# VectorE computes 1024 rank-one updates of the MLP's second product, and GpSimd makes the low parts of the MLP's weights

## The chip, the cores and the metric

The kernel runs on one core of one Trainium2 chip. The metric is the device time of one execution in microseconds (us), as the median of several runs. The engines are TensorE (PE, with its weight loads shown as PEld), VectorE (DVE), ScalarE (ACT), GpSimd (POOL) and SyncE (SP), whose queue issues nearly all of this kernel's DMAs.

## The reference

One decoder layer is applied to 256 prompt positions and 8 x 4 sampled positions, 288 tokens in all, with 2048 channels and float32 data:

```
h = rmsnorm(x)
proj = h @ w_in + b_in                    # 2048 -> 3072
mix = concat(conv group, pooling group)   # 1024 + 1024
x = x + mix @ w_out                       # 2048 -> 2048
h2 = rmsnorm(x)
f = square(relu(h2 @ w_ff1))              # 2048 -> 8192
x = x + f @ w_ff2                         # 8192 -> 2048
y = rmsnorm(x)
```

New convolution and pooling states are outputs too. The change touches the last two products, the MLP.

## The kernel before

Channels lie on the 128 partitions and the 288 tokens (`T`) along the free dimension. `xT` holds the residual x as 16 blocks of 128 x 288.

A float32 product is made of three TensorE products of rounded parts. Each operand is split into a high part and a low part (the remainder), and `product` (L279 to L284) adds high x high, high x low and low x high into one PSUM bank. The weights are split while they stream in. `split` (L270 to L277) takes a raw tile of 128 x 1024 numbers (four weight blocks for each of two output blocks), lets ScalarE copy it to the high part `whi` (L275), and lets an engine that the caller names subtract to get the low part `wlo` (L276). `weight_groups` (L308) names that engine. In the first stages, the input projection, the pooling product and the first half of the output product, it is GpSimd (`G`). In the second half of the output product and in the whole MLP it is VectorE (`V`, L327 and L329).

A `gemm` (L286) makes two output blocks of 128 channels from 16 blocks of input channels: 16 x 2 products of three matmuls, 96 matmuls of 128 x 288, and four weight tiles. The pool of raw tiles holds six, the pools of `whi` and `wlo` four each, so the split of a tile for the next gemm waits until PE has read the tile that lay in its place. PSUM gives the gemms four banks, two for each, so a gemm can start once the bank pair of the gemm before the last has been read.

The MLP (L565) has four chunks of 2048 hidden channels. A chunk is eight gemms of the first product (FF1) and eight of the second (FF2). After an FF1 gemm, VectorE makes `t` from the bank (L574), ScalarE squares it into `f` (L576) and copies the high part `fh`, and VectorE makes `fl` (L579). After an FF2 gemm, VectorE adds the two banks to their blocks of `xT` (L589, the function `evict`). Between the output product and the MLP, GpSimd splits a row of sums (`parts`, L232 and L233, into `th` and `tl`) for the second norm.

The order of instructions on each engine is set by a scheduler when the program is built. It simulates the engines and takes, of what is ready, what has the lowest priority number. Code inside `with later():` gets a number a million higher, so it is placed where its engine would otherwise have nothing to do. All DMAs of weights are issued from the one queue of SP, in order, and each waits there until its raw tile is free.

Of the kernel before, what the change touches and what calls it, by code (L numbers as in the profile page):

```python
# [9 lines left out]
F32 = mybir.dt.float32  # L10
F32R = mybir.dt.float32r
AF = mybir.ActivationFunctionType
ALU = mybir.AluOpType
# [3 lines left out]
P = 128  # L17
# [3 lines left out]
T = SEQ + NB * NS  # L21
# [8 lines left out]
N8 = DC // P  # L30
WINDOWS = (2, 4, 8, 16)
FCH = 2048
US = CH + NS
UO = CH + SEQ
UL = UO + NB * US
ZS = PH + NS
# [5 lines left out]

GROUPS = (3, 2, 1, 0)
SEQUENCE = [("conv", i) for i in range(2, 7)] + [("pool", 3), ("pool", 2), ("pool", 1), ("mix", 3), ("pool", 0), ("mix", 2), ("conv", 7)]


def weight_blocks():

    def w_in(*cols):
        return [("w_in", r, cols) for r in range(0, D, 1024)]  # L50

    a, b = [w_in(i * P, DC + i * P) for i in range(2)]
    yield from (a[0], b[0], a[1], b[1])
    for kind, i in SEQUENCE:
        if kind == "mix":
            if i == 3:
                yield "pool_w", 0, (0, P)
            continue
        yield from w_in(i * P, DC + i * P) if kind == "conv" else w_in(2 * DC + 2 * i * P, 2 * DC + (2 * i + 1) * P)
    for r in (DC, 0):  # L60
        for c in range(0, D, 256):
            yield "w_out", r, (c, c + P)
    for ch in range(0, DFF, FCH):
        for c in range(ch, ch + FCH, 256):
            for r in range(0, D, 1024):
                yield "w_ff1", r, (c, c + P)
        for c in range(0, D, 256):
            for r in range(ch, ch + FCH, 1024):
                yield "w_ff2", r, (c, c + P)
# [12 lines left out]
def trunk_kernel(ctx: ExitStack, tc: tile.TileContext, io):  # L82
    nc = tc.nc
# [5 lines left out]
    actp = ctx.enter_context(tc.tile_pool(name="actp", bufs=40))  # L89
    tmpp = ctx.enter_context(tc.tile_pool(name="tmpp", bufs=6))  # L90
    prdp = ctx.enter_context(tc.tile_pool(name="prdp", bufs=1))
    acc = ctx.enter_context(tc.tile_pool(name="acc", bufs=4, space=PSUM))
    cvp = ctx.enter_context(tc.tile_pool(name="cvp", bufs=2, space=PSUM))
    msp = ctx.enter_context(tc.tile_pool(name="msp", bufs=2, space=PSUM))
# [7 lines left out]
    @contextmanager  # L102
    def later(by=LATER):

        tc.cur_priority += by
        yield
        tc.cur_priority -= by

    def row(name):
        return rowp.tile([P, T], F32, name=nm(name), tag="row")  # L110
# [4 lines left out]
    def act(name, **kw):  # L115
        return slot(name, F32R, **(kw or {"tag": "act"}))
# [4 lines left out]
    def ms(name, n=512):  # L121
        return msp.tile([P, n], F32, name=nm(name), tag="ms", padded_shape=[P, 512])
# [17 lines left out]
    xT = const.tile([P, KT, T], F32, name="xT")  # L140
    uz = const.tile([P, N8 * (UL + ZL)], F32, name="uz")
# [12 lines left out]
    def load():  # L154

        src = io["w"][next(next_block)]
        raws = []
        for h in range(2):
            raw = raw_tile()
            nc.sync.dma_start(raw, src[:, 4 * h : 4 * h + 4, :])  # L160
            raws.append(raw)
        return raws
# [107 lines left out]
    def split(raw, eng, cuts=((0, 4),)):  # L270

        hi = wspl.tile([P, 4, 256], F32R, name=nm("whi"), tag="whi")
        lo = wspl.tile([P, 4, 256], F32R, name=nm("wlo"), tag="wlo")
        for a, b in cuts:
            nc.scalar.copy(hi[:, a:b, :], raw[:, a:b, :])  # L275
            eng.tensor_tensor(lo[:, a:b, :], raw[:, a:b, :], hi[:, a:b, :].bitcast(F32), op=ALU.subtract)  # L276
        return hi, lo  # L277

    def product(bank, rhs, w, first, last):  # L279

        (xh, xl), (wh, wl), b = rhs, w, bank[:, :T]
        nc.tensor.matmul(b, wh, xh, start=first, stop=False)  # L282
        nc.tensor.matmul(b, wh, xl, start=False, stop=False)  # L283
        nc.tensor.matmul(b, wl, xh, start=False, stop=last)  # L284

    def gemm(banks, rhs, m_outer=False, hooks={}):  # L286

        n = len(rhs)
        get = ready.pop()
        order = [(k, m) for k in range(n) for m in range(len(banks))]  # L290
        if m_outer:
            order.sort(key=lambda km: km[1])
        for j, (k, m) in enumerate(order):
            hooks.get(j, bool)()
            product(banks[m], rhs[k], get(k, m), k == 0, k == n - 1)
        ready.extend(itertools.islice(weights, 1))

    korder = [2 * g + m for g in GROUPS for m in range(2)]
# [1 line left out]
    def halves(parts, at=lambda k: k):  # L300

        def get(k, m):
            k = at(k)
            return tuple(t[:, k % 4, m * P : (m + 1) * P] for t in parts[k // 4])

        return get

    def weight_groups():  # L308

        V, G = nc.vector, nc.gpsimd  # L310
        def mix(g):

            return halves(parts, lambda k: 2 * g + k)

        for kind, i in SEQUENCE:
            if kind == "mix":
                if i == 3:
                    parts = [split(raw, G) for raw in load()]
                yield mix(i)
            else:  # L320
                yield halves([split(raw, G) for _ in range(2) for raw in load()])
        yield mix(1)
        yield mix(0)
        for _ in range(8):
            yield halves([split(raw, G) for raw in load()], lambda k: korder[k])
        for _ in range(8):
            yield halves([split(raw, V) for raw in load()])  # L327
        for _ in range(2 * DFF // 256):
            yield halves([split(raw, V) for _ in range(2) for raw in load()])  # L329

    weights = weight_groups()
    ready = []
# [15 lines left out]
    for c in range(8):  # L348
# [5 lines left out]
        for k0, k1 in steps:  # L354
# [5 lines left out]
            if len(steps) == 2:  # L360
                r, h, l = [t[:, :, k0, :] for t in views]
            else:
                r, h, l = first_raw[c], hi, lo
# [27 lines left out]
    def conv_gates(i, bk):  # L391

        up = u_all[:, i, 0:UO]
        us = samples(u_all[:, i, UO:UL], US)
        a, g = bk[0][:, :T], bk[1][:, :T]
# [4 lines left out]
        if i == N8 - 1:  # L400
            load_table(AF.Sqrt, tg[:, 0:1])
        for out, a, b in ((up[:, CH:UO], a[:, :SEQ], tg[:, :SEQ]), (us[:, :, CH:US], samples(a[:, SEQ:T], NS), samples(tg[:, SEQ:T], NS))):
            nc.vector.scalar_tensor_tensor(out=out, in0=a, scalar=v("b_in", i), in1=b, op0=ALU.add, op1=ALU.mult)
# [80 lines left out]
    conv_taps((0, 1))  # L484
    for kind, i in SEQUENCE:
        (conv_group if kind == "conv" else mix_group if kind == "mix" else pool_group)(i)
# [42 lines left out]
    for g in range(8):  # L529
        bk = bank2()  # L530
# [10 lines left out]
    for g in range(8):  # L541
        bk = bank2()
        gemm(bk, mixc)
        for m in range(2):
            k = 2 * g + m
# [9 lines left out]
            else:  # L555
                q2 = bank("q", cvp, "cv")[:, :T]
                nc.scalar.activation(q2, xk, AF.Square)
                nc.vector.tensor_tensor(ss2, ss2, q2, op=ALU.add)

    r2 = row("r2")  # L560
    ss2 = parts(ss2)
    pss = ms("pss")
    ssf = row("ssf")
    pf = ms("pf", 8)
    for ch in range(DFF // FCH):  # L565
        fx = []
        for g in range(FCH // 256):
            bk = bank2()
            gemm(bk, x1, hooks={4: lambda: column_sum(pss, ones_r, ss2)} if ch == 0 and g == 0 else {})
            if ch == 0 and g == 0:  # L570
                rsqrt_wide(pss, r2, 1.0 / D)
            for m in range(2):
                t = tmp("t")
                nc.vector.scalar_tensor_tensor(out=t, in0=bk[m][:, :T], scalar=0.0, in1=r2, op0=ALU.max, op1=ALU.mult)  # L574
                f = tmp("f")
                nc.scalar.activation(f, t, AF.Square)  # L576
                fh, fl = act("fh"), act("fl")
                nc.scalar.copy(fh, f)
                nc.vector.tensor_tensor(fl, f, f32(fh), op=ALU.subtract)  # L579
                fx.append((fh, fl))  # L580
        last = ch == DFF // FCH - 1
        for g in range(8):
            bk = bank2()

            def evict(m):

                k = 2 * g + m
                xk = xT[:, k, :]
                nc.vector.tensor_tensor(xk, xk, bk[m][:, :T], op=ALU.add)  # L589
                if last:  # L590
                    if k == 0:
                        nc.scalar.activation(ssf, xk, AF.Square)
                    else:
                        qf = tmp("q")
                        nc.scalar.activation(qf, xk, AF.Square)
                        if k < KT - 1:
                            nc.vector.tensor_tensor(ssf, ssf, qf, op=ALU.add)
                        else:
                            token_sum(pf, qf, first=False)
                    nc.scalar.activation(xk, xk, AF.Copy, scale=v("norm_f", k))  # L600

            if last and g == 7:
                gemm(bk, fx, m_outer=True, hooks={16: lambda: evict(0), 28: lambda: token_sum(pf, ssf, last=False)})
            else:
                gemm(bk, fx)
                evict(0)
            evict(1)

    rf = rsqrt_rows(pf, 1.0 / D)
    for k0, n in ((0, 1), (1, 2), (3, 4), (7, 4), (11, 3), (14, 2)):  # L610
# [61 lines left out]
```

## Time and profile before

| | |
|---|---|
| median of 3 runs | 1081.23 us (1081.09 to 1081.39) |
| profiled execution | 1081.47 us, span 1079.5 us, mean granted TensorE clock 0.995 |
| PE | 1066.4 us busy, 8176 matmuls |
| DVE | 634.7 us busy, of it 333.3 us in 272 low parts of weights (L276) |
| ACT | 470.9 us busy, of it 344.9 us in 330 high parts (L275) |
| POOL | 164.6 us busy, of it 138.5 us in 58 low parts; idle from 272.3 us on |
| DMA | 187.04 MB, the queues' packets take 54% of the 16 engines' span |

The MLP begins at about 266 us of the span. A matmul's record lasts 291 ns, but the records overlap: one starts every 130 ns. In the same way a DVE record begins a little before the one ahead of it ends. So the cost of an instruction in a row of equal ones is read from start to start, not from its record.

### The profile page before, as it was taken

To read this page: it belongs to the slowest core of one execution; us is meant where nothing else is said; L and a number is where in the kernel's file an instruction comes from. 1 tells how busy PE (TensorE), PEld (TensorE's weight loads), DVE (VectorE), ACT (ScalarE), POOL (GpSimd) and SP (SyncE) were. 2 spreads that over 40 slices of the span, in tenths; PEclk is the share of its full clock that TensorE was granted. 3 is DMA by queue.
4 is the path that set the end of the run, shared out by engine and by line. 5 is a ranking of instruction groups with operands and counts; after the bars stand their busy time and mean duration, and the time that the engine had idled before them with its cause. 6 is when DMAs were issued, how large, how long until landed. Compare 5 with 4: busy or idle time off the path is not lost.

```text
span 1079.5 us, 19710 instructions
## 1 busy us (share of the span) xinstructions
PE 1066.4 (99%) x8176; PEld 1065.0 (99%) x8176; DVE 634.7 (59%) x983; ACT 470.9 (44%) x649; POOL 164.6 (15%) x110
## 2 busy tenths in 40 slices
PE   9999999999999999999999999999999999999995
PEld 9999999999999999999999999999999999999995
DVE  7799999687745544445554444555444455555453
ACT  7544454575444433334443333444333334444441
POOL 0899888500000000000000000000000000000000
PEclk9999999999999999999999999999999999999997
DMA  9655577555555555555555555555555555545522
GB/s 336 225 184 176 178 197 214 169 170 166 172 164 170 175 168 165 175 163 171 173 166 169 173 163 172 171 165 174 171 163 174 164 170 175 166 166 176 163 92 88
DMA packets 56649, 187.04 MB, mean 173 GB/s; under 512 B 5872, under 2 KB 11504, under 8 KB 56560
## 3 DMA queue, kind: packets, MB, share of 16 engines
q1 hardware_dynamic: 56416, 185.74, 53.6%
q8 instruction: 64, 1.05, 0.4%
q14 instruction: 25, 0.20, 0.1%
q10 hardware_dynamic: 144, 0.05, 0.0%
HBM read 181.49 MB, written 4.28 MB: 172 GB/s over the span
## 4 chain that ended last, share of the span: by engine, by line
PE 98%; DVE 1%; DMA 0%; ACT 0%; SPq 0%; DVEq 0%; issue 0%
PE ac L282 32%; PE ac L283 32%; PE ac L284 32%; PE ac L371 1%; PE cv L371 1%; DMA xT<-in_xT 0%; DVE xT L612 0%; PE pr L267 0%; PE pf L227 0%; ACT hh L357 0%; SPq L168 0%; SPq L175 0%; DVEq L658 0%; ACT uz L341 0%; PE m L284 0%
## 5 line engine op out<-in xcount | busy, mean ns | idle before, releaser
L275 ACT CAST whi<-wr 128x1024 fp32r<-128x1024 f32 x330 | 344.9, 1046 | 570.3 <-PE ac L283 538.0
L276 DVE TENSOR_TENSOR wlo<-wr,whi 128x1024 fp32r<-128x1024 f32 x272 | 333.3, 1225 | 361.2 <-ACT whi L275 361.1
L282 PE MATMUL ac<-fh,whi 128*128 128x288 f32 x1024 | 298.2, 291 | 0.0
L283 PE MATMUL ac<-al,whi 128*128 128x288 f32 x1024 | 298.1, 291 | 0.0
L284 PE MATMUL ac<-ah,wlo 128*128 128x288 f32 x1024 | 298.1, 291 | 0.0
L283 PE MATMUL ac<-fl,whi 128*128 128x288 f32 x1024 | 298.1, 291 | 0.0
L284 PE MATMUL ac<-fh,wlo 128*128 128x288 f32 x1024 | 298.1, 291 | 0.0
L282 PE MATMUL ac<-ah,whi 128*128 128x288 f32 x1024 | 298.1, 291 | 0.0
L283 PEld LDWEIGHTS ac<-fl,whi 128*128 128x128 f32 x1024 | 191.7, 187 | 0.0
L283 PEld LDWEIGHTS ac<-al,whi 128*128 128x128 f32 x1024 | 191.7, 187 | 0.0
L282 PEld LDWEIGHTS ac<-fh,whi 128*128 128x128 f32 x1024 | 191.7, 187 | 0.0
L284 PEld LDWEIGHTS ac<-ah,wlo 128*128 128x128 f32 x1024 | 191.7, 187 | 0.0
L282 PEld LDWEIGHTS ac<-ah,whi 128*128 128x128 f32 x1024 | 191.7, 187 | 0.0
L284 PEld LDWEIGHTS ac<-fh,wlo 128*128 128x128 f32 x1024 | 191.7, 187 | 0.0
L276 POOL TENSOR_TENSOR wlo<-wr,whi 128x1024 fp32r<-128x1024 f32 x58 | 138.5, 2413 | 20.6 <-ACT whi L275 20.6
L424 DVE SCALAR_TENSOR_TENSOR pc<-uz,vec,pc 128x256 f32<-128x256 f32 x232 | 98.8, 483 | 5.3 <-ACT pc L413 3.5
L282 PE MATMUL ac<-hh,whi 128*128 128x288 f32 x320 | 92.1, 292 | 0.0
L283 PE MATMUL ac<-hl,whi 128*128 128x288 f32 x320 | 92.1, 291 | 0.0
L284 PE MATMUL ac<-hh,wlo 128*128 128x288 f32 x320 | 87.3, 291 | 0.0
L282 PEld LDWEIGHTS ac<-hh,whi 128*128 128x128 f32 x320 | 59.9, 187 | 0.0
L283 PEld LDWEIGHTS ac<-hl,whi 128*128 128x128 f32 x320 | 59.9, 187 | 0.0
L284 PEld LDWEIGHTS ac<-hh,wlo 128*128 128x128 f32 x320 | 57.8, 187 | 0.0
(159 smaller groups left out, 877.2 us busy)
## 6 DMA issues: line engine op xcount, KB each, us to landing
wr<-in_w SPq DMA_DIRECT2D x336, 512.0 KB, 3.7
out_u_out<-uz SPq DMA_DIRECT2D x1, 1208.0 KB, 9.6
xT<-in_xT SPq DMA_DIRECT2D x2, 576.0 KB, 8.3
out_yT<-xT SPq DMA_DIRECT2D x2, 576.0 KB, 2.9
uz<-in_hist_c SPq DMA_DIRECT2D x1, 1088.0 KB, 11.6
wr<-in_w SPq DMA_DIRECT2D x4, 256.0 KB, 5.1
xT<-in_xT SPq DMA_DIRECT2D x3, 288.0 KB, 5.8
out_z_out<-uz SPq DMA_DIRECT2D x1, 668.0 KB, 7.6
```

The source lines that it names most:

```text
L275: nc.scalar.copy(hi[:, a:b, :], raw[:, a:b, :])
L276: eng.tensor_tensor(lo[:, a:b, :], raw[:, a:b, :], hi[:, a:b, :].bitcast(F32), op=ALU.subtract)
L282: nc.tensor.matmul(b, wh, xh, start=first, stop=False)
L283: nc.tensor.matmul(b, wh, xl, start=False, stop=False)
L284: nc.tensor.matmul(b, wl, xh, start=False, stop=last)
L371: nc.tensor.matmul(first_banks[m][:, :T], lhs(w, k, m), pair[k][x], start=c == 0 and k == 0 and w is hi and x == 0, stop=c == 7 and k == 1 ...
L424: nc.vector.scalar_tensor_tensor(out=dst, in0=u_all[:, i, w : w + SEQ], scalar=cw[i][:, w : w + 1], in1=pc[i], op0=ALU.mult, op1=ALU.add)
```

## The change

There are two edits.

**Low parts.** `weight_groups` passes `G` where it passed `V` for the 64 weight groups of the MLP: 256 subtractions of 128 x 1024 go from VectorE to GpSimd. The 16 of the second half of the output product stay on VectorE.

**Held products.** The first chunk's FF2 multiplies 16 blocks of `f` with the weights. For the first of these blocks and the first eight output blocks (`BY`), the product leaves TensorE: the first four FF2 gemms of chunk 0 begin at block 1 instead of 0 (`begin`), which is 4 x 2 products of three matmuls, 24 matmuls. VectorE makes the same product in float32 as 128 x 8 rank-one updates, one for each hidden channel k of the block and each output block m: `xT[m] = f[k] * w[k, m] + xT[m]`, an instruction `scalar_tensor_tensor` over 128 x 288. For that

- the eight weight blocks are loaded again with output channels on the partitions (`turn`: 32 DMAs with runs of 32 numbers, then 8 transposes on VectorE), into the place where the conv and pooling inputs lay (`uz`), which is free once the two state outputs have been stored;
- `f` of the first FF1 gemm's first block is stored to a DRAM tile `fd` by one DMA from SP, and comes back in 32 DMAs of four rows, each of them sent to all 128 partitions (`partition_broadcast`), into five places (`HELD`) used in turn;
- the updates are given out 20 at a time (`PACE`) after each gemm of the MLP by `advance`, with the priority of `later`.

```
-            yield halves([split(raw, V) for _ in range(2) for raw in load()])
+            yield halves([split(raw, G) for _ in range(2) for raw in load()])
...
-    def gemm(banks, rhs, m_outer=False, hooks={}):
+    def gemm(banks, rhs, m_outer=False, hooks={}, begin=0):
...
-        order = [(k, m) for k in range(n) for m in range(len(banks))]
+        order = [(k, m) for k in range(begin, n) for m in range(len(banks))]
...
-            product(banks[m], rhs[k], get(k, m), k == 0, k == n - 1)
+            product(banks[m], rhs[k], get(k, m), k == begin, k == n - 1)
...
+    def turn():
+        with later():
+            for m in range(BY):
+                src = io["w"][first_ff2() + 2 * (m // 2)][:, 0, (m % 2) * P : (m % 2 + 1) * P]
+                for j in range(4):
+                    nc.sync.dma_start(
+                        blocks[32 * j : 32 * j + 32, m, :].rearrange("r (i c) -> r i c", c=32),
+                        src[:, 32 * j : 32 * j + 32].rearrange("(i r) c -> r i c", r=32),
+                    )
+                nc.vector.transpose(turned[:, m, :], blocks[:, m, :])
+
+    def held_products():
+        with later():
+            for b in range(P // ROWS):
+                at = held_rows[:, b % HELD]
+                nc.sync.dma_start(at, fd[b * ROWS : (b + 1) * ROWS, :].partition_broadcast(P))
+                for m in range(BY):
+                    for r in range(ROWS):
+                        k = b * ROWS + r
+                        nc.vector.scalar_tensor_tensor(out=xT[:, m, :], in0=at[:, r, :], scalar=turned[:, m, k : k + 1], in1=xT[:, m, :], op0=ALU.mult, op1=ALU.add)
+                        yield
...
+    def advance():
+        for _ in range(PACE):
+            next(macs, None)
...
+                if ch == 0 and g == 0 and m == 0:
+                    nc.sync.dma_start(fd, f)
...
+            advance()
...
-                gemm(bk, fx)
+                gemm(bk, fx, begin=1 if ch == 0 and 2 * g < BY else 0)
```

The scheduler decides where the updates stand. On VectorE, the stretch around the first FF2 gemms of chunk 0 read before (`wlo` is a low part, an L589 row adds a bank to `xT`):

```order
L276 TENSOR_TENSOR wlo_4803<-wr_4798,whi_4802 128x1024
L589 TENSOR_TENSOR xT<-xT,ac_4688 128x288
L589 TENSOR_TENSOR xT<-xT,ac_4689 128x288
L276 TENSOR_TENSOR wlo_4807<-wr_4800,whi_4806 128x1024
L276 TENSOR_TENSOR wlo_4915<-wr_4910,whi_4914 128x1024
L276 TENSOR_TENSOR wlo_4919<-wr_4912,whi_4918 128x1024
L276 TENSOR_TENSOR wlo_4927<-wr_4922,whi_4926 128x1024
L589 TENSOR_TENSOR xT<-xT,ac_4812 128x288
```

Four low parts stand between the evictions of one gemm and those of the next. In the changed kernel an L593 row is updates and an L637 row is an eviction, and the same stretch reads:

```order
L593 SCALAR_TENSOR_TENSOR xT<-uz,xT 128x288 x14
L637 TENSOR_TENSOR xT<-xT,ac_5036 128x288
L593 SCALAR_TENSOR_TENSOR xT<-uz,xT 128x288
L637 TENSOR_TENSOR xT<-xT,ac_5037 128x288
L593 SCALAR_TENSOR_TENSOR xT<-uz,xT 128x288 x24
L637 TENSOR_TENSOR xT<-xT,ac_5175 128x288
L593 SCALAR_TENSOR_TENSOR xT<-uz,xT 128x288
L637 TENSOR_TENSOR xT<-xT,ac_5176 128x288
L593 SCALAR_TENSOR_TENSOR xT<-uz,xT 128x288 x25
```

The four low parts have gone, and 25 updates stand in their place, one of them between the two evictions of a gemm. Counted from one gemm's evictions (or its two `t`) to the next one's, 43 gemms of the chunks 0 to 2 have 9 to 28 updates behind them, 1024 in all; the last two or three FF1 gemms of the chunks 1 and 2 and all of chunk 3 have none.

After FF1 gemms, in the same engine's queue, the updates stand between `t` (L619) and `fl` (L626); these rows are from the second and third gemm of chunk 0:

```order
L619 SCALAR_TENSOR_TENSOR t_3909<-ac_3787,r_3609 128x288
L593 SCALAR_TENSOR_TENSOR xT<-uz,xT 128x288 x8
L619 SCALAR_TENSOR_TENSOR t_3917<-ac_3788,r_3609 128x288
L593 SCALAR_TENSOR_TENSOR xT<-uz,xT 128x288 x3
L626 TENSOR_TENSOR fl_3914<-f_3911,fh_3913 128x288
L593 SCALAR_TENSOR_TENSOR xT<-uz,xT 128x288 x7
L626 TENSOR_TENSOR fl_3922<-f_3919,fh_3921 128x288
L593 SCALAR_TENSOR_TENSOR xT<-uz,xT 128x288 x7
L619 SCALAR_TENSOR_TENSOR t_4068<-ac_3946,r_3609 128x288
```

Before, only low parts stood between them. GpSimd's queue ended before with the row of sums of the second norm:

```order
L276 TENSOR_TENSOR wlo_2858<-wr_2853,whi_2857 128x1024
L276 TENSOR_TENSOR wlo_2862<-wr_2855,whi_2861 128x1024
L232 CAST th_3567<-ss_2931 128x288
L233 TENSOR_TENSOR tl_3568<-ss_2931,th_3567 128x288
L658 UNCONDITIONAL_BRANCH
```

In the changed kernel it goes on (L283 is the low part, L239 and L240 are the sums' parts):

```order
L283 TENSOR_TENSOR wlo_2864<-wr_2857,whi_2863 128x1024
L283 TENSOR_TENSOR wlo_3533<-wr_3528,whi_3532 128x1024
L283 TENSOR_TENSOR wlo_3537<-wr_3530,whi_3536 128x1024
L283 TENSOR_TENSOR wlo_3545<-wr_3540,whi_3544 128x1024
L283 TENSOR_TENSOR wlo_3549<-wr_3542,whi_3548 128x1024
L239 CAST th_3610<-ss_2933 128x288
L283 TENSOR_TENSOR wlo_3722<-wr_3717,whi_3721 128x1024
L240 TENSOR_TENSOR tl_3611<-ss_2933,th_3610 128x288
L283 TENSOR_TENSOR wlo_3726<-wr_3719,whi_3725 128x1024
```

The low parts of the first MLP gemm and one of the second now stand ahead of the sums' second part, and 251 more follow behind it.

More of the change, by code (lines that the diff above doesn't have):

```diff
@@ L32 @@
 FCH = 2048
+BY, ROWS, HELD, PACE = 8, 4, 5, 20
 US = CH + NS
@@ L44, with first_ff2 @@
 SEQUENCE = [("conv", i) for i in range(2, 7)] + [("pool", 3), ("pool", 2), ("pool", 1), ("mix", 3), ("pool", 0), ("mix", 2), ("conv", 7)]
+def first_ff2():
+    return next(j for j, b in enumerate(weight_blocks()) if b[0] == "w_ff2")
 def weight_blocks():
@@ L91, in trunk_kernel @@
     prdp = ctx.enter_context(tc.tile_pool(name="prdp", bufs=1))
+    held = ctx.enter_context(tc.tile_pool(name="held", bufs=1, space=bass.MemoryType.DRAM))
     acc = ctx.enter_context(tc.tile_pool(name="acc", bufs=4, space=PSUM))
@@ L558, in trunk_kernel @@
                 nc.vector.tensor_tensor(ss2, ss2, q2, op=ALU.add)
+    turned = uz[:, 0 : BY * P].rearrange("p (m k) -> p m k", k=P)
+    blocks = uz[:, BY * P : 2 * BY * P].rearrange("p (m k) -> p m k", k=P)
+    held_rows = uz[:, 2 * BY * P : 2 * BY * P + HELD * ROWS * T].rearrange("p (h r t) -> p h r t", h=HELD, t=T)
+    fd = held.tile([P, T], F32, name="fd")
+    def turn():
[18 more added lines that the diff above has]
+                        yield
+    macs = held_products()
+    turn()
     r2 = row("r2")
@@ L604, in trunk_kernel @@
             else:
-                gemm(bk, fx)
+                gemm(bk, fx, begin=1 if ch == 0 and 2 * g < BY else 0)
                 evict(0)
             evict(1)
+            advance()
     rf = rsqrt_rows(pf, 1.0 / D)
```

## The prediction

> **What bounds the kernel now.** I read the page's busy times, then the middle of the MLP by windows, then VectorE's timeline there. The first line is of the page; the second is a row of the windows, whose columns are the length, then for each engine busy us (x instructions), the granted clock, DMA share and GB/s.
>
> ```profile
> PE 1066.4 (99%) x8176; PEld 1065.0 (99%) x8176; DVE 634.7 (59%) x983; ACT 470.9 (44%) x649; POOL 164.6 (15%) x110
> 300.00:1040.00 740.00, 740.00 (x5694) 740.00 (x5693) 366.41 (x425) 295.61 (x377) 0.00 (x0) 1.00 0.53 169
> ```
>
> TensorE has no gap in 740 us and runs at the full clock: 740/5694 = 0.130 us from matmul to matmul, so 96 x 0.130 = 12.48 us for a gemm. POOL is idle there, DVE half idle. VectorE's timeline (start, us, instruction) shows the same beat in the evictions, 428.30 and 440.78:
>
> ```profile
> 428.30 0.84 DVE L589 TENSOR_TENSOR xT<-xT,ac 128x288 f32<-128x288 f32 x2 [0.56 <-PE ac L284]
> 429.64 1.23 DVE L276 TENSOR_TENSOR wlo<-wr,whi 128x1024 fp32r<-128x1024 f32 x1 [0.49 <-ACT whi L275]
> 432.76 1.23 DVE L276 TENSOR_TENSOR wlo<-wr,whi 128x1024 fp32r<-128x1024 f32 x1 [1.89 <-ACT whi L275]
> 435.88 1.22 DVE L276 TENSOR_TENSOR wlo<-wr,whi 128x1024 fp32r<-128x1024 f32 x1 [1.89 <-ACT whi L275]
> 439.00 1.23 DVE L276 TENSOR_TENSOR wlo<-wr,whi 128x1024 fp32r<-128x1024 f32 x1 [1.90 <-ACT whi L275]
> 440.78 0.84 DVE L589 TENSOR_TENSOR xT<-xT,ac 128x288 f32<-128x288 f32 x2 [0.56 <-PE ac L284]
> ```
>
> So TensorE is the bound, with no more to hide: any time taken from its list is won, and any wait put into it is lost. What decides is whether VectorE and GpSimd can do the new work within 12.48 us a gemm.
>
> **What the change takes from TensorE.** 24 matmuls at 0.130 us: -3.1 us. That is the whole gain.
>
> **What it puts on the two other engines.** The prices of single instructions, from the groups by form and from VectorE's timeline:
>
> ```profile
> L276 POOL TENSOR_TENSOR wlo<-wr,whi 128x1024 fp32r<-128x1024 f32 x58 | 138.5, 2413 | 20.6 <-ACT whi L275 20.6
> L276 DVE TENSOR_TENSOR wlo<-wr,whi 128x1024 fp32r<-128x1024 f32 x272 | 333.3, 1225 | 361.2 <-ACT whi L275 361.1
> L589 DVE TENSOR_TENSOR xT<-xT,ac 128x288 f32<-128x288 f32 x64 | 27.1, 454 | 25.7 <-PE ac L284 25.7
> L579 DVE TENSOR_TENSOR fl<-f,fh 128x288 fp32r<-128x288 f32 x64 | 26.3, 452 | 0.0
> L551 DVE SCALAR_TENSOR_TENSOR al<-xT,vec,ah 128x288 fp32r<-128x288 f32 x16 | 8.1, 513 | 0.0
> 330.94 0.82 DVE L579 TENSOR_TENSOR fl<-f,fh 128x288 fp32r<-128x288 f32 x2
> 262.08 0.51 DVE L551 SCALAR_TENSOR_TENSOR al<-xT,vec,ah 128x288 fp32r<-128x288 f32 x1
> 262.51 0.45 DVE L558 TENSOR_TENSOR ss<-ss,q 128x288 f32<-128x288 f32 x1
> ```
>
> GpSimd: four low parts a gemm, 4 x 2.41 = 9.6 us of 12.48. A gemm's low part is wanted about 9 us after its place comes free (three of four tiles later), and ScalarE's copy and GpSimd's 2.4 us fit in that. Alone, GpSimd keeps up.
>
> VectorE: the update has the form of `al`, two tensors in SBUF with a scalar by partition, 128 x 288: record 0.513 us, start to start 262.51 - 262.08 = 0.43 us. 1024 of them are 440 us. They are spread over 43 gemms, 23.8 each, with up to 28 (the order shown ahead). With 28 that is 12.0 us, and two evictions at 0.84 - 0.45 = 0.39 us (two records less one) make 12.8. Alone, VectorE is about as full as TensorE, and nothing is left over.
>
> **Together they don't run side by side.** In the kernel before GpSimd does its low parts only where VectorE's instructions read one of their inputs from PSUM. The one place where a GpSimd subtraction meets a VectorE instruction with both inputs in SBUF is at 270 us:
>
> ```profile
> L429 POOL TENSOR_TENSOR sum_c<-sum_c,c x7: 808/811/844, 81.9 to 192.9; 128x288 f32<-128x288 f32 x7
> L276 POOL TENSOR_TENSOR wlo<-wr,whi x58: 2383/2405/2454, 30.8 to 203.4; 128x1024 fp32r<-128x1024 f32 x58
> 270.12 0.42 POOL L232 CAST th<-ss 128x288 fp32r<-128x288 f32 x1 [64.28 <-DVE ss L558]
> 270.62 1.67 POOL L233 TENSOR_TENSOR tl<-ss,th 128x288 fp32r<-128x288 f32 x1
> 270.30 1.33 DVE L276 TENSOR_TENSOR wlo<-wr,whi 128x1024 fp32r<-128x1024 f32 x1 [0.31 <-ACT whi L275]
> ```
>
> The first two rows (min/median/max ns) are GpSimd's subtractions and sums elsewhere; the first has the shape of `tl` and takes 0.81 us, and no low part takes more than 2.45. `tl` took 1.67, 0.86 longer, and it lay under VectorE's low part from 270.62 to 271.63, 1.01 us. So GpSimd stood still for 85% of the overlap, and VectorE's own instruction, which began under `th`, took 1.33 instead of 1.23. A control, GpSimd full for 50 us under VectorE's convolution taps, whose `pc` is in PSUM:
>
> ```profile
> 60.00:110.00 50.00, 50.00 (x387) 50.00 (x386) 46.17 (x113) 21.55 (x29) 50.00 (x25) 1.00 0.53 170
> L276 POOL TENSOR_TENSOR wlo<-wr,whi 128x1024 fp32r<-128x1024 f32 x18 | 42.9, 2434 | 0.0
> L424 DVE SCALAR_TENSOR_TENSOR pc<-uz,vec,pc 128x256 f32<-128x256 f32 x88 | 36.0, 482 | 2.8 <-ACT pc L413 2.8
> ```
>
> Both have their usual lengths there (2434 against 2413 ns, 482 ns for a 256 column tap). The new updates are of the bad kind: `uz` and `xT` are both in SBUF, and so are `f` and `fh` of `fl`. I therefore take it that an update and a low part exclude each other, and the two engines' times add.
>
> [...]
>
> **The sum.** Over the 43 gemms that have updates:
>
> - updates 1024 x 0.43 = 440 us
> - low parts 43 x 4 x 2.405 = 414 us
> - `fl` of 19 FF1 gemms, 38 x 0.37 (0.82 - 0.45) = 14 us
> - evictions and `t`, 86 x 0.39 = 34 us
>
> together 902 us, against 43 x 12.48 = 537 us on TensorE: +365 us. VectorE may lag a gemm before TensorE misses a bank, and the updates come in three stretches (chunk 0 with the start of chunk 1, and two more): -3 x 12.5 = -37 us. With -3.1 the profiled 1081.5 us becomes **1406 us**; the profiled execution is 0.2 us above the median, which I neglect.
>
> [...] From 452 ns for 288 and 1225 for 1024 columns it streams 1.05 ns a column, 0.302 us: 1024 x 0.128 = 131 us less. GpSimd by the same slope (811 and 2405 ns, 2.17 ns a column) holds 2.22 us: 32 us less. That gives 1243. If each update stands by itself at 0.513 us, it is 85 us more, 1491. I take 0.43 and 2.405, as the one overlap lost nearly all of its length.
>
> **The small parts.** The DMAs:
>
> ```profile
> wr<-in_w SPq DMA_DIRECT2D x336, 512.0 KB, 3.7
> out_u_out<-uz SPq DMA_DIRECT2D x1, 1208.0 KB, 9.6
> L494 SPq DMA_DIRECT2D out_u_out<-uz x1: 582/582/582, 163.5 to 163.5; - x1
> ```
>
> The 32 reloads wait in SP's queue for the state output to land (9.6 us), with the weights of the output product behind them, and take about 32 x 0.58 = 19 us to issue. Six raw tiles at two per gemm of 48 matmuls, 6.2 us, are a lead of some 18 us less 3.7 of landing: 0 to 14 us lost, I take 0. The 32 broadcasts move 128 x 4.6 KB, about one weight tile each, at a DMA share of 0.53; five places are five gemms of lead: nothing. The one store of `f` holds SP for a few us, with `wr` tiles behind it that are wanted a gemm later: nothing. In GpSimd's queue one low part now stands between `th` and `tl`; `t` of the first gemm has a whole gemm of room: nothing. The 8 transposes fall where VectorE is half idle.
>
> **The rivals.**
>
> *They don't hinder each other.* Then VectorE's 12.8 us at most a gemm against 12.48, with a gemm of lead, stay hidden, and 1081.5 - 3.1 = 1078.4 us is faster. For it: the control at 60 to 110 us. Against it: `tl`. It decides if updates keep 0.43 us beside low parts of 2.4. Chance 0.05.
>
> *VectorE alone is the bound*, or the hindrance is slight: updates at 0.513 us make a gemm with 24 of them 12.3 + 0.74 + 0.78 = 13.8 us, with 27 14.6: about 1.8 x 40 - 37 = 35 us more, 1113; with a part of the hindrance up to 1240. Chance 0.09.
>
> *GpSimd is starved.* If VectorE's row of updates never lets a low part in, TensorE waits for weights, VectorE then for TensorE's gemm, and each gemm costs the sum plus the last tile's 3.12 us: 43 x 3.12 = 134 us more, 1540. Chance 0.08.
>
> *TensorE's clock falls.* At the end of the kernel, where TensorE waits in short turns, the granted clock was 0.78 and 0.50:
>
> ```profile
> 1066.00:1070.00 4.00, 2.09 (x12) 1.94 (x12) 0.90 (x6) 1.24 (x3) 0.00 (x0) 0.78 0.00 0
> 1070.00:1079.00 9.00, 0.18 (x1) 0.00 (x0) 5.28 (x6) 0.00 (x0) 0.00 (x0) 0.50 0.66 262
> ```
>
> If it stayed at half, a gemm would take 25 us, more than the 21 of the sum: 1078.4 + 43 x 12.48 = 1615 us. It didn't stay down where matmuls follow each other without a break (1.00 in the windows quoted above), and a gemm is 12 us of that; chance 0.04. [...]
>
> **How the numbers follow.** The forecast has 0.74, its own range is 1243 to 1491. To leave out no more than 2 in 10 I take in the starved case and the upper edge of the slight one: 1220 to 1550. What can be told from no change is 0.2%. Faster: 0.05, the second way. Same: 0.01, its edge. Slower: 0.94.
>
> **What would show it.** In the chunks 0 to 2 TensorE has gaps, ended by VectorE's evictions; low parts on POOL or updates on DVE have records far above 2.41 and 0.51 us, and sum to some 20 us a gemm; chunk 3 has the old 12.48 us beat and the time lost is all before it. It is wrong if both keep their lengths, or if TensorE waits for weights (`wlo`) or DMA instead.

## The result: 28% slower

| | before | changed |
|---|---|---|
| median | 1081.16 us (1081.09 to 1081.39, 4 runs) | 1382.93 us (1380.54 to 1384.14, 4 runs) |
| span of the profiled execution | 1079.5 us | 1381.2 us |
| mean granted TensorE clock | 0.995 | 0.903 |

The ratio is 1.279, 95% interval 1.2775 to 1.2805. The page of the changed kernel, its busy times, the slices of 1/40 of the span for PE, DVE and POOL, and the chain of waits by engine:

```profile
PE 1137.3 (82%) x8152; PEld 1122.8 (81%) x8152; DVE 1152.6 (83%) x1759; ACT 472.4 (34%) x649; POOL 876.1 (63%) x366
PE   9999999997767766687789765677897657999996
DVE  6999977769999999999988999999869999412333
POOL 1998870275655757756558655565586567577772
DVE 52%; PE 38%; issue 6%; POOL 3%; DMA 1%; ACT 1%; SPq 0%; DVEq 0%; POOLq 0%; ACTq 0%
```

TensorE, full before, has gaps from the tenth slice on, and the chain that sets the end now runs mostly over VectorE. The main waits of TensorE between 285 and 1155 us (waiter, what ended the wait, us in total, times, longest):

```profile
PE ac L289 <- DVE xT L637: 129.4, 15, 14.2
PE ac L289 <- DVE t L619: 52.6, 21, 4.5
PE ac L291 <- POOL wlo L283: 13.9, 8, 2.8
```

It waits for PSUM banks that VectorE hasn't read yet, and far less for weights (13.9 us for low parts, 9.8 us for high parts). The stretches of the MLP, windows of one FF1 or FF2 each (chunks 0 and 1, then chunk 3):

```profile
270.80:404.20 133.40, 111.32 (x772) 109.01 (x770) 120.12 (x163) 43.53 (x60) 82.56 (x33) 0.90 0.46 152
404.20:561.30 157.10, 109.84 (x746) 107.42 (x746) 157.10 (x223) 38.63 (x43) 103.31 (x32) 0.84 0.38 129
561.30:717.40 156.10, 116.43 (x769) 113.33 (x769) 154.46 (x214) 41.76 (x59) 87.36 (x33) 0.85 0.42 136
717.40:861.80 144.40, 106.73 (x770) 105.66 (x769) 134.83 (x182) 36.01 (x39) 99.07 (x34) 0.87 0.39 129
1152.10:1267.00 114.90, 103.08 (x770) 102.68 (x769) 48.91 (x66) 42.75 (x60) 80.53 (x34) 0.94 0.49 155
1267.00:1367.40 100.40, 100.40 (x775) 100.20 (x773) 28.87 (x33) 43.40 (x63) 70.01 (x30) 1.00 0.40 127
```

Each took 100 us before. In FF2 of chunk 0 VectorE has no idle moment in 157 us. The loss stands where updates are; in the last stretch, which has none, the 100 us are back, with GpSimd at 70 us of work. All eight stretches together took 1096.6 us instead of 799.7. TensorE was busy for 869.3 of them, so 227 us of the loss are gaps and about 70 us are matmuls at the lower clock, 0.84 to 0.94 in the windows with gaps. The groups of the two kinds of instruction, by the page, and the spread of their records (min/median/max ns):

```profile
L283 POOL TENSOR_TENSOR wlo<-wr,whi 128x1024 fp32r<-128x1024 f32 x314 | 850.4, 2728 | 453.3 <-ACT whi L282 444.5
L593 DVE SCALAR_TENSOR_TENSOR xT<-uz,xT 128x288 f32<-128x288 f32 x1024 | 774.8, 824 | 3.9 <-DMA uz<-fd 3.8
L283 POOL TENSOR_TENSOR wlo<-wr,whi x314: 2352/2456/9037, 30.9 to 1355.5; 128x1024 fp32r<-128x1024 f32 x157
L593 DVE SCALAR_TENSOR_TENSOR xT<-uz,xT x1024: 498/506/2697, 298.0 to 1181.5; 128x288 f32<-128x288 f32 x171
```

The median update is as short as forecast, 0.51 us, but some take 2.7, a low part's length, and the mean is 0.82. A low part takes up to 9 us. How that comes about is seen in the two engines' timelines at 400 to 420 us (start, us, instruction, count; the POOL rows are of two narrower windows):

```profile
405.86 0.44 DVE L619 SCALAR_TENSOR_TENSOR t<-ac,r 128x288 f32<-128x288 f32 x1
406.23 3.50 DVE L593 SCALAR_TENSOR_TENSOR xT<-uz,xT 128x288 f32<-128x288 f32 x8
409.66 0.44 DVE L619 SCALAR_TENSOR_TENSOR t<-ac,r 128x288 f32<-128x288 f32 x1
410.03 7.37 DVE L593 SCALAR_TENSOR_TENSOR xT<-uz,xT 128x288 f32<-128x288 f32 x3
417.32 2.65 DVE L626 TENSOR_TENSOR fl<-f,fh 128x288 fp32r<-128x288 f32 x1
419.89 3.08 DVE L593 SCALAR_TENSOR_TENSOR xT<-uz,xT 128x288 f32<-128x288 f32 x7
...
426.27 0.45 DVE L619 SCALAR_TENSOR_TENSOR t<-ac,r 128x288 f32<-128x288 f32 x1
```

```profile
408.27 3.69 POOL L283 TENSOR_TENSOR wlo<-wr,whi 128x1024 fp32r<-128x1024 f32 x1 [8.60 <-ACT whi L282]
412.07 5.01 POOL L283 TENSOR_TENSOR wlo<-wr,whi 128x1024 fp32r<-128x1024 f32 x2
```

Up to 409.66 VectorE runs its eight updates at 0.43 us each, and the low part that GpSimd begins at 408.27 takes 3.69 us instead of 2.4: it ends at 411.96, 2.30 us after VectorE's `t` began, about what a low part takes alone, so by these times it got nowhere before. `t` reads a bank in PSUM, and from 410.03 on the two take turns: three updates need 7.37 us, one for each low part, and `fl` takes 2.65. Once GpSimd has nothing left, seven updates need 3.08 us again. It is the same in other gemms: all 23 low parts longer than 2.9 us in this trace end 2.28 to 2.35 us after the start of a `t` or of an eviction. From `t` to `t` the gemm took 20.4 us instead of 12.5.

### The profile page after: what moved, and what is told of

Same layout as the page of the kernel before. It is cut to its first block, busy times and chain, and to the rows that moved or that the text cites. A ratio compares the mean times of both kernels' runs of the same rounds, so it can differ in the third digit from the quotient of the medians.

```text
span 1381.2 us, 20762 instructions
## 1 busy us (share of the span) xinstructions
PE 1137.3 (82%) x8152; PEld 1122.8 (81%) x8152; DVE 1152.6 (83%) x1759; ACT 472.4 (34%) x649; POOL 876.1 (63%) x366
## 4 chain that ended last, share of the span: by engine, by line
DVE 52%; PE 38%; issue 6%; POOL 3%; DMA 1%; ACT 1%; SPq 0%; DVEq 0%; POOLq 0%; ACTq 0%
DVE xT L593 47%; PE ac L291 12%; PE ac L289 12%; PE ac L290 12%; POOL wlo L283 3%; DVE fl L626 2%; DVE xT L637 1%; PE ac L378 1%; PE cv L378 1%; DVE t L619 1%; DMA uz<-fd 0%; DVE xT L661 0%; DMA xT<-in_xT 0%; PE pr L274 0%; DVE r L257 0%
## 5 line engine op out<-in xcount | busy, mean ns | idle before, releaser
L283 POOL TENSOR_TENSOR wlo<-wr,whi 128x1024 fp32r<-128x1024 f32 x314 | 850.4, 2728 | 453.3 <-ACT whi L282 444.5
L593 DVE SCALAR_TENSOR_TENSOR xT<-uz,xT 128x288 f32<-128x288 f32 x1024 | 774.8, 824 | 3.9 <-DMA uz<-fd 3.8
L289 PE MATMUL ac<-ah,whi 128*128 128x288 f32 x1024 | 318.3, 311 | 95.3 <-DVE t L619 47.1
L291 PE MATMUL ac<-ah,wlo 128*128 128x288 f32 x1024 | 314.3, 308 | 12.4 <-POOL wlo L283 12.4
L290 PE MATMUL ac<-al,whi 128*128 128x288 f32 x1024 | 314.0, 307 | 0.0
L289 PEld LDWEIGHTS ac<-ah,whi 128*128 128x128 f32 x1024 | 207.9, 203 | 101.5 <-issue 54.8
L290 PEld LDWEIGHTS ac<-al,whi 128*128 128x128 f32 x1024 | 208.0, 203 | 0.0
L621 ACT ACTIVATE f<-t 128x288 f32<-128x288 f32 x64 | 27.0, 440 | 253.8 <-DVE t L619 253.8
L626 DVE TENSOR_TENSOR fl<-f,fh 128x288 fp32r<-128x288 f32 x64 | 75.0, 1189 | 19.0 <-ACT fh L625 19.0
L637 DVE TENSOR_TENSOR xT<-xT,ac 128x288 f32<-128x288 f32 x64 | 27.6, 446 | 74.2 <-PE ac L291 74.2
```

The lines of the kernel that those rows point to most:

```text
L593: nc.vector.scalar_tensor_tensor(out=xT[:, m, :], in0=at[:, r, :], scalar=turned[:, m, k : k + 1], in1=xT[:, m, :], op0=ALU.mult, op1=ALU.add)
```

## The experiments

All are variants of the two kernels. Times are medians, each against the kernel before on the same chip. "Port theory" in the expectations is the name of the prediction's assumption that such an update and a low part exclude each other; no run shows a port.

**The low parts alone.** Is GpSimd too slow for the MLP by itself? The kernel before with

```
-            yield halves([split(raw, V) for _ in range(2) for raw in load()])
+            yield halves([split(raw, G) for _ in range(2) for raw in load()])
```

> The kernel before with one edit: GpSimd makes the low parts of the MLP's weights, and no product is held. Port theory (a VectorE instruction with two SBUF inputs and a GpSimd subtraction exclude each other): GpSimd has 9.6 us of a 12.48 us gemm, VectorE's only such instructions are two subtractions fl of 0.45 us after an FF1 gemm, so both fit and the time stays within 0.2% of 1081.2 us, with some fl stretched to over 2 us. Rival (GpSimd is simply too slow or too late for the MLP): TensorE waits for low parts, and a large part of the 302 us is already here.

Measured: 1081.31 us against 1080.94, ratio 1.0004 (0.9994 to 1.0013). Nothing is lost. `fl`, the one VectorE instruction of the first three chunks with both inputs in SBUF, shows the meeting (min/median/max ns), and the window of the MLP shows that there is room for it:

```profile
L579 DVE TENSOR_TENSOR fl<-f,fh x64: 446/1124/2431, 285.1 to 968.8; 128x288 fp32r<-128x288 f32 x64
300.00:1040.00 740.00, 740.00 (x5694) 740.00 (x5694) 127.76 (x189) 295.66 (x378) 569.38 (x238) 1.00 0.53 169
```

**The products alone.** The changed kernel with that line as it was before, so that VectorE keeps its 256 low parts and GpSimd is idle.

> The changed kernel with the low parts of the MLP left on VectorE, so GpSimd is idle in the MLP and VectorE has more to do than in the changed kernel: 1024 updates at 0.43 us, plus four low parts of 1.15 us a gemm. Port theory: faster than the changed kernel by far, although VectorE's list grows by 256 instructions; by VectorE's own sum, 440 + 43 x 4 x 1.15 + 14 + 34 = 686 us against 537 of TensorE less 40, some 1165 to 1195 us, and every update has its 0.51 us record. Rival (VectorE is overloaded by the updates alone, or the broadcasts and reloads on the DMA queue are the cause): 1383 us or more.

Measured: 1167.38 us against 1080.94, ratio 1.080 (1.0778 to 1.0821). With more instructions on VectorE the kernel is 216 us faster than the changed one, and its updates are all short:

```profile
L593 DVE SCALAR_TENSOR_TENSOR xT<-uz,xT x1024: 496/508/539, 300.5 to 1051.0; 128x288 f32<-128x288 f32 x171
```

So the long records belong to the meeting of the two engines, and broadcasts, reloads and VectorE's own length explain at most 86 us. Most of these 86 are VectorE's length: the time stands at the lower edge of the sum that was expected, and TensorE waits 67.7 us for evictions, the longest 21. The MLP also begins 4.3 us later than before.

**The same updates with one input in PSUM.** The changed kernel with

```
+    sums = [bank("hp", cvp, "cv")[:, :T] for _ in range(2)]
+    for s in sums:
+        nc.vector.memset(s, 0.0)
     macs = held_products()
...
-nc.vector.scalar_tensor_tensor(out=xT[:, m, :], in0=at[:, r, :], ..., in1=xT[:, m, :], ...)
+nc.vector.scalar_tensor_tensor(out=sums[m % 2], in0=at[:, r, :], ..., in1=sums[m % 2], ...)
```

> The changed kernel with the updates adding into two PSUM banks (cleared before) instead of into x: each update then has one input in SBUF and one in PSUM. Same number of updates, same loads, low parts on GpSimd. It leaves out adding these sums to x. Port theory: updates and low parts run side by side, the records of both keep 0.5 and 2.4 us, and nearly all of the 302 us is gone: 1078 to 1115 us (at 24 to 26 updates a gemm VectorE is just within 12.48 us). Rivals (VectorE's load, the broadcasts, the order in SP's queue): nothing of that has changed, 1350 us or more.

Measured: 1083.43 us against 1080.94, ratio 1.0027 (1.0016 to 1.0038). Of the 302 us, 299 are gone, with the same number of updates, the same DMAs and the same low parts on GpSimd. The run leaves out adding the sums to `xT`; runs that add them follow below. The spread of the updates and of the low parts, and the window:

```profile
L593 DVE SCALAR_TENSOR_TENSOR hp<-uz,hp x1024: 500/511/521, 298.4 to 808.1; 128x288 f32<-128x288 f32 x171
L283 POOL TENSOR_TENSOR wlo<-wr,whi x314: 2374/2402/2747, 30.8 to 1055.2; 128x1024 fp32r<-128x1024 f32 x157
300.00:1040.00 740.00, 739.75 (x5691) 739.55 (x5690) 546.63 (x1212) 306.16 (x383) 575.71 (x239) 1.00 0.60 194
```

The edit moves two things to PSUM, the update's second input and its result. Which of them counts is seen in the run with the low parts alone, where GpSimd is busy for 569 of 740 us: `t` and the evictions read one input from a bank and write their result to SBUF, and none of them is stretched (min/median/max ns), while `fl` is.

```profile
L574 DVE SCALAR_TENSOR_TENSOR t<-ac,r x64: 447/458/459, 283.7 to 965.1; 128x288 f32<-128x288 f32 x64
L589 DVE TENSOR_TENSOR xT<-xT,ac x64: 453/453/455, 378.2 to 1065.5; 128x288 f32<-128x288 f32 x64
```

So a result in SBUF did no harm in this run (0.45 us beside low parts with a median of 2.40), and what remains as the cause of the stretched records is that VectorE's second input lies in SBUF. The MLP itself is 2.6 us shorter than before (270.1 to 1067.2 against 266.0 to 1065.7 us), of the 3.1 forecast; it begins 4.1 us later, of which below.

**Half the updates.** The changed kernel with `BY, ROWS, HELD, PACE = 4, 4, 5, 20`.

> The changed kernel with four output blocks instead of eight: 512 updates and 12 matmuls, 16 reloads instead of 32, but the same 32 broadcasts, and about the same 24 to 28 updates behind a gemm for half as many gemms. Port theory: the cost goes with the gemms that have updates, 22 instead of 43 at some 7 us each, 1225 to 1245 us. If the broadcasts were the cause it would stay near 1380 us.

Measured: 1233.4 us against 1080.94, ratio 1.141 (1.1387 to 1.1433): 152 us lost for 512 updates, 302 for 1024. The broadcasts, as many as before, are not the cause.

**A faster version, first two tries.** If the 24 matmuls are to be won, updates and low parts must not meet. Either VectorE keeps the low parts and there are fewer updates (the transposed weights are laid out by the host and come by one DMA in place of the reloads and transposes),

```
-BY, ROWS, HELD, PACE = 8, 4, 5, 20
+BY, ROWS, HELD, PACE = 6, 4, 5, 14
...
+            nc.sync.dma_start(turned, io["turned"])
...
+        "turned": a["w_ff2"][0][:P, : BY * P].reshape(P, BY, P).transpose(2, 1, 0),
```

> The changed kernel with the low parts on VectorE, six output blocks instead of eight (768 updates, 18 matmuls fewer), and the transposed weight blocks laid out by the host and loaded by one DMA, so the 32 reloads and the 8 transposes are gone. GpSimd is idle in the MLP, so nothing contends. By VectorE's sum a gemm with 14 to 16 updates has 16 x 0.43 + 4 x 1.15 + 0.8 = 12.3 us of 12.48, which the one gemm of lead should cover: 1081.0 - 18 x 0.13 = 1078.6 us. If VectorE's list is a little too long, TensorE waits for evictions as it did with 1024 updates: 1080 to 1095 us.

or the updates add in PSUM, four blocks at a time:

```
+            sums = [bank("hp", cvp, "cv")[:, :T] for _ in range(2)] + [ms("hp")[:, :T] for _ in range(2)]
+            for p in range(0, BY, 4):
...
+                nc.vector.scalar_tensor_tensor(out=sums[m], in0=at[:, r, :], scalar=turned[:, p + m, k : k + 1], in1=sums[m], op0=ALU.mult, op1=ALU.add)
...
+                for m in range(4):
+                    nc.vector.tensor_tensor(xT[:, p + m, :], xT[:, p + m, :], sums[m], op=ALU.add)
```

> The changed kernel with the updates adding into four PSUM banks, in two passes of four output blocks (the rows are broadcast twice, 64 DMAs), each pass ending with four additions of a bank to x; the transposed weight blocks are laid out by the host and loaded by one DMA. GpSimd makes the low parts of the MLP. Nothing of the product is left out. Port theory: 24 to 26 updates a gemm run beside the low parts, TensorE has no gap, and the 24 matmuls are won: 1081.0 - 3.1 = 1077.9 us. If the doubled broadcasts or VectorE's length cost something, 1080 to 1100 us. If the hindrance were not bound to the inputs' place, above 1300 us.

Measured: 1085.57 us against 1080.93, ratio 1.0039 (1.0026 to 1.0052), and 1094.67 us (1088.90 to 1097.79), ratio 1.0118 (1.0095 to 1.0141). Both miss the time expected. In both the MLP begins on time (266.1 and 265.6 us), so the later start belongs to the reloads and transposes. In both nearly all is lost in chunk 0. In the first, TensorE has one wait there:

```profile
PE ac L289 <- DVE xT L629: 3.5, 1, 3.5
```

It stands behind the last FF1 gemm, where the schedule put 28 updates and eight low parts together. The window of the MLP has 53 matmuls fewer than the kernel before (5694):

```profile
300.00:1040.00 740.00, 736.08 (x5641) 735.68 (x5640) 674.54 (x1187) 300.98 (x376) 0.00 (x0) 1.00 0.59 191
```

53 matmuls at 0.130 us are 6.9 us. Only 3.9 us of the window are gaps; the other 3.0 went to matmuls that start more than 0.130 us apart.

The profiled execution of the second, 1088.90 us, was the fastest of its runs, so what the others lost beyond it isn't seen. In it, a window in FF1 and FF2 of chunk 0 shows VectorE without rest and TensorE with gaps; a window of chunk 1 shows none (windows):

```profile
335.00:385.00 50.00, 44.33 (x323) 42.65 (x322) 50.00 (x104) 21.11 (x31) 35.19 (x16) 0.97 0.68 223
485.00:585.00 100.00, 100.00 (x771) 100.00 (x771) 79.22 (x173) 45.75 (x65) 77.27 (x33) 1.00 0.71 229
```

A full VectorE alone is not enough for that: the run that added in two banks had no pace either, and no such gap. The second try also sends each row twice, and one update there waited 4.7 us for its broadcast. What each of the two costs was not separated.

**With a pace.** The scheduler takes updates as soon as they are ready, whatever `advance` gives out. So the updates of each `advance` were queued behind the last instruction of their gemm on VectorE:

```
+        with tc.issue_after(ins.ins):
             for _ in range(PACE):
                 next(macs, None)
```

with four output blocks and ten updates a gemm for the first way, eight blocks and 20 for the second.

> The kernel with the low parts on VectorE and the host's layout of the transposed blocks, with four output blocks (512 updates, 12 matmuls fewer), and with each ten updates put in VectorE's order behind the last instruction of the gemm that gives them out, so that no gemm has more than about ten (the schedule alone put 28 and 8 low parts behind the last FF1 gemm of chunk 0, where TensorE then waited 3.8 us). By VectorE's sum a gemm has 10 x 0.43 + 4 x 1.15 + 0.74 + 0.78 = 10.4 us of 12.48: TensorE has no gap, 1080.9 - 12 x 0.13 = 1079.4 us. If the lead isn't the cause of those gaps: 1081 to 1086 us.

> The two passes into four PSUM banks with the low parts on GpSimd, with each twenty updates put in VectorE's order behind the last instruction of the gemm that gives them out. VectorE then has 20 x 0.43 + 0.74 + 0.78 = 10.1 us of a 12.48 us gemm instead of up to 12.3, and a broadcast has more time. If the gaps in chunk 0 (11 us, behind updates that waited for a broadcast and a VectorE without rest) came from VectorE's full list, they go: 1080.9 - 3.1 = 1077.8 us. If the doubled broadcasts are too much for the DMA engines beside the weights: 1085 us or more.

Measured: 1079.94 us against 1080.93, ratio 0.9990 (0.9981 to 0.9999), and 1081.45 us, ratio 1.0009 (1.0000 to 1.0018). The first has no gap left in the MLP but a wait of 0.3 us. In the second one gap of 1.8 us remained, at 343 us. ScalarE's timeline before it:

```profile
338.51 0.45 ACT L619 ACTIVATE f<-t 128x288 f32<-128x288 f32 x1 [8.38 <-DVE t L617]
340.14 3.88 ACT L282 CAST whi<-wr 128x1024 fp32r<-128x1024 f32 x4
```

ScalarE stood 8.38 us at `f`, whose `t` lay behind 17 updates on VectorE, and four high parts had gathered behind it. The first gemms with updates had 24 of them, not 20. The last run takes 19 updates and lets them begin two gemms later:

```
-BY, ROWS, HELD, PACE = 8, 4, 5, 20
+BY, ROWS, HELD, PACE = 8, 4, 5, 19
...
+            if ch or g > 1:
+                advance(done)
```

> The paced two passes into PSUM with 19 updates a gemm instead of 20 and the first of them given out two gemms later. In the run before, three of the first gemms had 24 updates, a t then stood behind 17 updates on VectorE, ScalarE's square waited 8.4 us for it with the high parts of the next weights behind it, and TensorE had its one gap, 2 us with a lower clock after it, 3.6 us in all. If that chain is the cause, no gap is left: 1080.9 - 3.1 = 1077.8 us, faster than both kernels. If the broadcasts beside the weights are the cause: about 1081 us again.

Measured: 1079.05 us (1078.45 to 1079.64) against 1081.21, ratio 0.9980 (0.9971 to 0.9989), 2.2 us faster than the kernel before, of the 3.1 hoped for. Whether 19 updates or the later begin did it was not separated. The window of its MLP, and GpSimd's low parts beside 1024 updates of 514 ns:

```profile
300.00:1040.00 740.00, 739.75 (x5691) 739.55 (x5690) 573.10 (x1230) 297.64 (x381) 571.53 (x239) 1.00 0.66 218
L589 DVE SCALAR_TENSOR_TENSOR hp<-uz,hp 128x288 f32<-128x288 f32 x1024 | 446.9, 514 | 2.3
L283 POOL TENSOR_TENSOR wlo<-wr,whi 128x1024 fp32r<-128x1024 f32 x314 | 753.0, 2404 | 251.0 <-ACT whi L282 250.9
```

The span was 2.7 us shorter (1076.8 against 1079.5). In this trace FF2 of chunk 0 took 3.1 us less, and about 0.4 us were lost at 973 us, where TensorE waits 0.3 us for a `t`; the rest of the missing 0.9 us stays open.

## Why the prediction was right, point by point

**TensorE's 3.1 us.** Right: without the meeting, FF2 of chunk 0 took 96.7 us instead of 99.8 (from its first matmul to the next chunk's) in the run with sums in PSUM and in the last run.

**Each engine alone keeps up.** Right for GpSimd (the low parts alone cost nothing). For VectorE it was said to be about as full as TensorE, and that is what the PSUM run shows: 1024 updates in 510 us with TensorE not held up. The tries for a faster version show the other side of "nothing left over": where the schedule put a few more, TensorE waited.

**The two exclude each other.** Right, and it was read from one subtraction that lost 0.86 us. The runs alone, together and with a PSUM input settle it. What the row of `tl` couldn't show, that a long GpSimd instruction holds up VectorE too, the changed kernel shows: updates of 2.7 us beside low parts of 2.4. And a row of updates, one behind the other, kept a low part out for several of them (it took 3.69 and up to 9.04 us instead of 2.4), until VectorE read a bank. In one point the prediction was too narrow: before, GpSimd's low parts met not only instructions with an input in PSUM, but also sums over a single input in SBUF (1.90 us each from 111 us on). They did no harm either: the four low parts from 112.16 us on took 9.52 us.

**The sum, 1406 us.** 23 us too high, inside its bounds. The term that was mis-sized is the update at 0.43 us: that holds while GpSimd is idle (24 took 10.37 us in the run with the products alone), but taking turns it added less. Two low parts from 412.07 on took 5.01 us; alone, three in a row took 7.12 in the kernel before (49.23 us there), so two take about 4.77:

```profile
49.23 7.12 POOL L276 TENSOR_TENSOR wlo<-wr,whi 128x1024 fp32r<-128x1024 f32 x3
```

The update between them added about 0.24 us, 0.2 less than assumed. For 43 x 4 low parts, an estimate, that is 33 us less. Whether the update or the low part gives way is not told apart. That would give 1373 us, 10 below the measured time; this rest stays open, and so do the 37 us taken off for VectorE's lag, which no run measured. The lower edge of the range, 1243 us, counts 0.302 us for an update and 2.22 us for a low part, estimates from the records of two shapes; no run shows either as the time in which one engine keeps the other out. What the trace shows in their place are the 0.24 us that the update added between two low parts.

**The starved case.** Partly there: GpSimd was kept out while updates followed each other (up to 9.04 us for a low part). But a `t` or an eviction broke the row in each gemm, low parts were still early enough, and TensorE waited only 13.9 us for them. The cost of the last tile that this case added did not arise.

**TensorE's clock.** It did fall, to 0.84 to 0.94 in the stretches with gaps. After a wait of 13.35 us that ended at 508.16, matmuls started every 0.24 us until 513.1, at a granted clock of 0.50, and every 0.13 us from there on (0.99 to 520 us): 4.9 slow us. In the 870 us from 285 to 1155 us VectorE waited only 20.6 us for TensorE (11.8 at evictions, 8.8 at `t`), so slow matmuls lay mostly under VectorE's list, and the 1615 us of a clock that stays at half did not come:

```profile
DVE xT L637 <- PE ac L291: 11.8, 2, 6.9
DVE t L619 <- PE ac L291: 8.8, 3, 6.9
```

**The small parts.** One was wrong. The reloads were priced at 0 to 14 us and taken as 0, and the transposes were put where VectorE is half idle. The MLP began 4.8 us late. It wasn't weights held up in SP's queue, as the price assumed: the transposes wait for their reloads in VectorE's own queue,

```profile
DVE uz L582 <- DMA uz<-in_w: 6.1, 4, 3.9
```

and the work of the conv group, which stands behind them, is late. At 196 us TensorE waits 0.9 us for a low part, as GpSimd had stood 3.85 us at a sum that needs VectorE's `c`. At 219 us it waits 1.67 us for the norm's result, and the granted clock in the window around it was 0.83 (1.00 there in the kernel before):

```profile
215.00:225.00 10.00, 8.33 (x52) 7.98 (x51) 8.63 (x23) 8.41 (x18) 0.00 (x0) 0.83 0.35 121
```

**What would show it.** Gaps ended by evictions, and both kinds of record stretched: as named. That chunk 3 keeps the old beat was half right: VectorE was so late that 34 updates ran in FF1 of chunk 3, which took 114.9 us.

## What to carry to other kernels

Before two engines are given work at the same time, look where each instruction's inputs lie: a VectorE instruction with both inputs in SBUF and a GpSimd subtraction took turns here (20 us a gemm instead of 12.5), while the same instruction adding in PSUM ran beside it at 0.51 us, with low parts of 2.40. A tuned kernel may simply never have let the two meet, so one odd duration in its trace, 1.67 us where 0.81 is usual, can be worth more than all averages. When an off-path engine is filled to nearly the beat of the bound, pace it by gemm. Pacing took the second try from 1094.67 us to 1081.45. Ten updates behind each gemm (beside four low parts on VectorE) or 19 (adding in PSUM) left TensorE with no gap above 0.3 us in the MLP, while one bunch of 28 with eight low parts cost a gap of 3.5 us.

## What was not expected

In the changed kernel a row of updates held GpSimd's low part out for as long as it went on (up to 9.04 us for one of 2.4); after a `t` or an eviction, which read PSUM, the two alternated one by one (three updates in 7.37 us). And a subtraction that met a low part was harmless where there was room: with the low parts alone on GpSimd, `fl` had a median of 1.12 us instead of 0.45, at no cost in time. Nor was a granted clock of 0.83 expected in the window of a 1.67 us wait.
